# Dividing the first x tile of an interleave kernel between two DMA queues: by columns or by partitions

## The chip, the cores and the metric

The kernel runs on one core of a Trainium2 chip. The metric is the device time of one launch in microseconds (us). Three runs of the kernel before took 314.11 to 314.35 us, with a median of 314.26 us.

## The reference

Two fp32 arrays, x and y, of shape (32, 256, 1024) are interleaved element by element along the last axis into one array of shape (32, 256, 2048):

```python
result = np.zeros((batch, seq, dim * 2), dtype=np.float32)
result[..., 0::2] = x
result[..., 1::2] = y
```

Each input has 33.55 MB and the output 67.11 MB, so 134.22 MB go between off-chip memory and the core. There is no arithmetic.

## The kernel before

Each input is seen as a flat array and cut into n = 8 tiles of 128 x 8192 elements (4 MiB): a tile is contiguous in memory, and row p of it, one partition, holds 8192 consecutive elements, 32 KiB. Since the interleave acts on the flat order, tile k of x and tile k of y give 128 rows of 16,384 output elements.

On-chip memory holds two x tiles (`xt0`, `xt1`), two y tiles (`yt0`, `yt1`) and two output tiles (`ot0`, `ot1`), each 128 x 8192. Output tile h takes half h of the columns: 4096 columns of x and 4096 of y, woven to 8192.

Three engines work, each through its own list, with counting semaphores between them. A DMA adds 16 to its semaphore when it has landed; a copy adds 1 to `woven`.

- SyncE (the SP queue) issues the loads (lines 47 to 55): for each k the x tile (line 52) and then the y tile (line 55). From k = 2 on it first waits until VectorE has read the old content of the buffer.
- VectorE (lines 57 to 70) takes, for each k and for h = 0 and 1, the x half-columns into the even places of `ot[h]` (line 67) and the y half-columns into the odd places (line 70). Before line 67 it waits for the x tile (`xsem`, only at h = 0) and from k = 1 on for the store that last read `ot[h]` (`osem`). Before line 70, at h = 0, it waits for the y tile (`ysem`).
- ScalarE (the ACT queue, lines 72 to 78) waits for each finished `ot[h]` and issues its store (line 76). The very first store is cut in two parts, 1 MiB and 3 MiB.

The first x tile is special. It is loaded by two DMAs, one from each queue (lines 45 and 46), which take one half of the columns of all 128 rows each: 128 pieces of 16 KiB. The part from the ACT queue has a semaphore of its own, `hsem`. VectorE waits for `xsem` before the first copy (h = 0), which needs only the first column half, and for `hsem` before the copy of the second (h = 1).

After the lists are built, `tile_interleave_kernel` takes the first DMA of SyncE and of ScalarE, which are these two, and moves them to the opening of the program, ahead of the barrier that the engines pass at the start.

Of the kernel before, what the change touches and what calls it, by code (L numbers as in the profile page):

```python
# [3 lines left out]


def _interleave(nc, x, y, out):
    P = 128
    W = 8192
    H = W // 2  # L10

    total = 1
    for s in x.shape:
        total *= s
    n = total // (P * W)
    assert n * P * W == total

    def rows(ap, names, k):
        flat = ap.rearrange("b s d -> (b s d)")
        return flat[k * names : (k + 1) * names].rearrange("(p w) -> p w", p=P)  # L20

    fp32 = mybir.dt.float32
    xt = [nc.alloc_sbuf_tensor(f"xt{b}", [P, W], fp32).ap() for b in (0, 1)]
    yt = [nc.alloc_sbuf_tensor(f"yt{b}", [P, W], fp32).ap() for b in (0, 1)]
    ot = [nc.alloc_sbuf_tensor(f"ot{b}", [P, W], fp32).ap() for b in (0, 1)]

    xsem = [nc.alloc_semaphore(f"xsem{b}") for b in (0, 1)]
    hsem = nc.alloc_semaphore("hsem")
    ysem = [nc.alloc_semaphore(f"ysem{b}") for b in (0, 1)]
    woven = nc.alloc_semaphore("woven")  # L30
    osem = [nc.alloc_semaphore(f"osem{b}") for b in (0, 1)]

    xs = [rows(x, P * W, k) for k in range(n)]
    ys = [rows(y, P * W, k) for k in range(n)]
    os_ = [rows(out, 2 * P * W, k) for k in range(n)]

    Q = W // 4

    def parts(k, h):
        return [slice(0, W)] if k or h else [slice(0, Q), slice(Q, W)]  # L40

    def stored(k, h):
        return 16 * sum(len(parts(j, h)) for j in range(k))

    nc.sync.dma_start(out=xt[0][:, :H], in_=xs[0][:, :H]).then_inc(xsem[0], 16)
    nc.scalar.dma_start(out=xt[0][:, H:], in_=xs[0][:, H:]).then_inc(hsem, 16)
    for k in range(n):
        b = k % 2
        if k >= 2:
            nc.sync.wait_ge(woven, 4 * (k - 2) + 3)  # L50
        if k:
            nc.sync.dma_start(out=xt[b], in_=xs[k]).then_inc(xsem[b], 16)
        if k >= 2:
            nc.sync.wait_ge(woven, 4 * (k - 2) + 4)
        nc.sync.dma_start(out=yt[b], in_=ys[k]).then_inc(ysem[b], 16)

    for k in range(n):
        b = k % 2
        for h in (0, 1):
            c = slice(h * H, (h + 1) * H)  # L60
            if h == 0:
                nc.vector.wait_ge(xsem[b], 16 * (k // 2 + 1))
            elif k == 0:
                nc.vector.wait_ge(hsem, 16)
            if k:
                nc.vector.wait_ge(osem[h], stored(k, h))
            nc.vector.tensor_copy(out=ot[h][:, 0::2], in_=xt[b][:, c]).then_inc(woven, 1)  # L67
            if h == 0:
                nc.vector.wait_ge(ysem[b], 16 * (k // 2 + 1))
            nc.vector.tensor_copy(out=ot[h][:, 1::2], in_=yt[b][:, c]).then_inc(woven, 1)  # L70

    for k in range(n):
        for h in (0, 1):
            nc.scalar.wait_ge(woven, 4 * k + 2 * h + 2)
            for c in parts(k, h):
                nc.scalar.dma_start(
                    out=os_[k][:, h * W : (h + 1) * W][:, c], in_=ot[h][:, c]
                ).then_inc(osem[h], 16)

    nc.scalar.wait_ge(osem[0], stored(n, 0))  # L80
    used = sorted(s.num for s in [*xsem, hsem, *ysem, woven, osem[0]])
    assert used == list(range(used[0], used[-1] + 1)), used
    nc.scalar.sem_clear(range(used[0], used[-1] + 1))
    nc.sync.nop(nofuse=True).wait_op(osem[1], stored(n, 1), "sem-ge").then_inc(
        osem[1], -stored(n, 1)
    )


def kernel(tc, x, y, out):
    nc = tc.nc  # L90
    tc.close()
    tc.compile()

    _interleave(nc, x, y, out)

    blocks = nc.main_func.blocks
    for engine in (mybir.EngineType.SP, mybir.EngineType.Activation):
        opening = blocks[0].instructions
        at, moved = next(
            (b, i)  # L100
            for b in blocks[1:]
            for i in b.instructions
            if i.engine == engine and i.opcode == "DMACopy"
        )
        assert not (moved.sync_info and moved.sync_info.on_wait)
        body = at.instructions
        body.remove(moved)
        gate = next(
            n
            for n, i in enumerate(opening)  # L110
            if i.engine == engine and i.opcode == "Drain"
        )
        opening.insert(gate, moved)
        at.instructions = body
        blocks[0].instructions = opening


# [1 line left out]
_INS = ['x', 'y']  # L119
_OUTS = [((32, 256, 2048), 'float32')]  # L120


# [23 lines left out]
```

## Time and profile before

| Item | Value |
|---|---|
| Median of 3 runs | 314.26 us (314.11 to 314.35) |
| The profiled execution, its own time | 314.21 us |
| Its span in the trace | 312.9 us |
| Busy time of VectorE | 71.9 us (23% of the span), 32 copies |
| A copy at line 67, at line 70 | 2295 ns, 2288 ns |
| Read and written by the DMA engines | 67.11 MB and 67.11 MB, 429 GB/s over the span |
| Chain that ended last | DMA 82%, DVE 12% |
| First store issued, last store issued | 24.35 us, 298.04 us |

The page cuts the span into 40 slices and gives each engine's busy share in tenths; the DMA row is the mean of the core's 16 DMA engines. The two DMA queues are q1, which has SyncE's loads, and q10, which has ScalarE's stores and one half of the first x tile. In the list of DMA issues, the time is from the issue to the landing of the whole transfer. In the timeline, a row of SPq or ACTq is the issue of a DMA and not its transfer. A view by stretches adds up bytes by whole packets, so that its GB/s and its DMA share can be some per cent off in a short stretch.

### The profile page before, as it was taken

The page shows a single profiled execution, that of the slowest core. Times are in us where ns is not written, and L with a number is a line of the kernel's source. Part 1 is how long each engine was busy: PE and PEld are TensorE (multiplying, and loading weights), DVE is VectorE, ACT ScalarE, POOL GpSimd, SP SyncE. Part 2 cuts the span into 40 slices and gives each one's busy share as a digit, 9 for nine tenths or more (in the row PEclk, how much of TensorE's full clock was granted, in tenths as well). Part 3 has the DMA queues.
Part 4 walks back from the last instruction along what each step waited for, and adds up shares of the span by engine and source line. Part 5 has one row for each costly group of instructions (what it writes and reads, how often), then busy time and mean ns, then how long its engine had stood idle before and what let it go on. Part 6 is the DMA issues. An engine that isn't in the chain of part 4 may idle for free.

```text
span 312.9 us, 114 instructions
## 1 busy us (share of the span) xinstructions
DVE 71.9 (23%) x32; POOL 0.2 (0%) x4
## 2 busy tenths in 40 slices
DVE  0216000501305023050230503205032050415400
POOL 0000000000000000000000000000000000000000
DMA  8999999999999999999999999999999999999998
GB/s 344 461 406 431 436 402 431 440 465 406 448 423 431 440 406 465 402 469 402 469 402 465 406 457 415 436 436 419 452 402 469 402 469 402 469 402 461 411 444 360
DMA packets 4896, 134.22 MB, mean 429 GB/s; under 512 B 544, under 2 KB 544, under 8 KB 544
## 3 DMA queue, kind: packets, MB, share of 16 engines
q10 hardware_dynamic: 2592, 69.21, 51.3%
q1 hardware_dynamic: 2304, 65.01, 48.5%
HBM read 67.11 MB, written 67.11 MB: 429 GB/s over the span
## 4 chain that ended last, share of the span: by engine, by line
DMA 82%; DVE 12%; issue 0%
DMA out_dram<-ot 76%; DMA yt<-in_y_dram 7%; DVE ot L70 6%; DVE ot L67 6%
## 5 line engine op out<-in xcount | busy, mean ns | idle before, releaser
L67 DVE COPY ot<-xt 128x4096 f32<-128x4096 f32 x16 | 36.7, 2295 | 218.0 <-DMA out_dram<-ot 206.3
L70 DVE COPY ot<-yt 128x4096 f32<-128x4096 f32 x16 | 36.6, 2288 | 8.0 <-DMA yt<-in_y_dram 8.0
L130 POOL MEMSET const-uint8-127<- 128x1 uint8 x1 | 0.1, 102 | 0.0
L130 POOL MEMSET const-bfloat16-1.0<- 128x1 bf16 x1 | 0.1, 101 | 0.0
L130 POOL MEMSET const-float32-0.0<- 128x1 f32 x1 | 0.1, 98 | 0.2 <-issue 0.2
L130 POOL MEMSET const-float32-1.0<- 128x1 f32 x1 | 0.1, 98 | 0.0
## 6 DMA issues: line engine op xcount, KB each, us to landing
out_dram<-ot ACTq DMA_DIRECT2D x15, 4096.0 KB, 34.1
yt<-in_y_dram SPq DMA_DIRECT2D x8, 4096.0 KB, 41.5
xt<-in_x_dram SPq DMA_DIRECT2D x7, 4096.0 KB, 24.4
out_dram<-ot ACTq DMA_DIRECT2D x1, 3072.0 KB, 32.8
xt<-in_x_dram SPq DMA_DIRECT2D x1, 2048.0 KB, 11.7
xt<-in_x_dram ACTq DMA_DIRECT2D x1, 2048.0 KB, 13.4
out_dram<-ot ACTq DMA_DIRECT2D x1, 1024.0 KB, 16.1
```

Source lines behind the costliest of these rows:

```text
L67: nc.vector.tensor_copy(out=ot[h][:, 0::2], in_=xt[b][:, c]).then_inc(woven, 1)
L70: nc.vector.tensor_copy(out=ot[h][:, 1::2], in_=yt[b][:, c]).then_inc(woven, 1)
L130: nc = _bacc.Bacc("TRN2", target_bir_lowering=False, num_devices=1)
```

## The change

The first x tile is still loaded by two DMAs, one from each queue, 2 MiB each, but the cut runs across the partitions: the SP queue's DMA takes rows 0 to 63 and the ACT queue's rows 64 to 127, each with whole rows of 32 KiB. Since the first copy (h = 0) reads all 128 rows, it now needs both DMAs, so the wait for `hsem` stands ahead of it, together with the wait for `xsem`; the wait ahead of the h = 1 copy goes.

```diff
-    nc.sync.dma_start(out=xt[0][:, :H], in_=xs[0][:, :H]).then_inc(xsem[0], 16)
-    nc.scalar.dma_start(out=xt[0][:, H:], in_=xs[0][:, H:]).then_inc(hsem, 16)
+    nc.sync.dma_start(out=xt[0][: P // 2], in_=xs[0][: P // 2]).then_inc(xsem[0], 16)
+    nc.scalar.dma_start(out=xt[0][P // 2 :], in_=xs[0][P // 2 :]).then_inc(hsem, 16)
...
             if h == 0:
                 nc.vector.wait_ge(xsem[b], 16 * (k // 2 + 1))
-            elif k == 0:
-                nc.vector.wait_ge(hsem, 16)
+                if k == 0:
+                    nc.vector.wait_ge(hsem, 16)
             if k:
                 nc.vector.wait_ge(osem[h], stored(k, h))
```

## The prediction

> **What bounds the kernel now.** I read the page first for who is busy, then the DMA rows, then the start of the timeline, the waits and the chain.
>
> From the page, the tenths of busy time and the queues:
>
> ```profile
> DVE  0216000501305023050230503205032050415400
> DMA  8999999999999999999999999999999999999998
> ...
> q10 hardware_dynamic: 2592, 69.21, 51.3%
> q1 hardware_dynamic: 2304, 65.01, 48.5%
> ```
>
> The 16 DMA engines are busy from the first slice to the last: the two queues' packets take 51.3 + 48.5 = 99.8% of the time that 16 engines have in the span. VectorE works 71.9 us of 312.9. So the kernel ends when 134.22 MB have gone through, and a lost DMA microsecond anywhere is a microsecond at the end. Next, what the DMA engines move per second (columns: stretch, its length, DVE busy, POOL busy, clock, DMA share, GB/s):
>
> ```profile
> 0.00:1.00 1.00, 0.00 (x0) 0.20 (x4) 1.00 0.07 16
> 1.00:3.00 2.00, 0.00 (x0) 0.00 (x0) 1.00 1.07 311
> 3.00:11.00 8.00, 0.00 (x0) 0.00 (x0) 1.00 1.01 432
> ...
> 100.00:290.00 190.00, 45.78 (x21) 0.00 (x0) 1.00 1.00 433
> ```
>
> Two things are to be seen. The stretch 3 to 11 us moves only the first x tile, in rows of 16 KiB, all loads; the stretch 100 to 290 us moves rows of 32 KiB, loads and stores mixed. Both run at 432 to 433 GB/s, which is 433 / 16 = 27.06 GB/s for each engine. Row length and direction do not matter; some path of fixed rate, one per engine, is full. And the start is slow: by 3.00 us, 16 + 2 x 311 = 638 KB have been moved where 433 GB/s would give 1299, so 661 KB, or 1.53 us, are lost there, about 1.0 us of it before the first byte.
>
> The start itself, from the timeline and the waits:
>
> ```profile
> 0.00 0.37 SPq L45 DMA_DIRECT2D xt<-in_x_dram  x1
> 0.12 0.37 ACTq L46 DMA_DIRECT2D xt<-in_x_dram  x1
> ...
> 11.70 2.30 DVE L67 COPY ot<-xt 128x4096 f32<-128x4096 f32 x1 [11.70 <-DMA xt<-in_x_dram]
> 22.02 2.29 DVE L70 COPY ot<-yt 128x4096 f32<-128x4096 f32 x1 [8.02 <-DMA yt<-in_y_dram]
> ```
>
> ```profile
> xt<-in_x_dram SPq DMA_DIRECT2D x1, 2048.0 KB, 11.7
> xt<-in_x_dram ACTq DMA_DIRECT2D x1, 2048.0 KB, 13.4
> ```
>
> The halves of the first x tile land at 11.7 and at 0.12 + 13.4 = 13.5 us. Each is 2.097 MB, or 4.84 us at 433 GB/s; had one been served whole before the other, it would have landed near 7 us. So the engines serve the two queues in turns, and both halves are in flight from end to end. The first y tile, issued third, lands at 22.0, and VectorE stands 8.0 us for it. The chain of waits starts with that transfer and is from there almost all stores:
>
> ```profile
> 1.57 20.43 DMA yt<-in_y_dram
> ...
> 28.75 48.06 DMA out_dram<-ot
> ```
>
> **The change, part by part.**
>
> *The wait on hsem moves from the second x copy to the first.* The first L67 copy now waits for both halves. In the present landing times it would start at 13.5 instead of 11.7 and end at 15.8. Queued behind it on VectorE is the first L70 copy, which cannot start before y lands at 22.0: 6.2 us of cover. If that cover were gone, the cost would be up to one copy, 2.3 us, in the first store; but even this would not reach the end by itself, because behind y the SP queue already holds the next x and y tiles, 8.39 MB or 19.4 us of work for the DMA engines. I cost it at nothing. The second L67 copy loses a wait that had long been met: nothing.
>
> *Rows of 32 KiB instead of 16.* 128 packets of the first x tile instead of 256, the same 4.194 MB. The two rows above give the same rate for both lengths: nothing in the steady flow. A gain can come only from the slow start; of its 1.53 us, 1.0 us precedes any data and is untouched, so the bound below nothing is 0.5 us. I take nothing.
>
> *Issue.* Two DMA issues as before, at the same places in the opening (the code that moves the first DMA of SP and ACT there takes the new ones alike): nothing.
>
> *Each transfer spans 64 rows instead of 128.* This is the cost that no row of the trace shows; every transfer in it spans all 128 rows. With 128 rows over 16 engines each engine has 8 rows; with 64, each has 4, and the 16 engines together address one half of the rows of on-chip memory. The measured limit of 27.06 GB/s can belong to the engine or to the path into its group of rows. The trace cannot part the two, as each engine has always had a group of rows to itself.
> - If it belongs to the engine, the 8 packets that each engine moves for this tile (4 from each queue) take 8 x 32,768 B / 27.06 GB/s = 8 x 1.211 = 9.69 us, as now. Cost: nothing.
> - If it belongs to the rows' path, a half has 8 paths for 16 engines. While all engines work on SP's half, two share each path and a packet takes 2.42 us; when all turn to ACT's half, the same holds of the other 8 paths, while the first 8 lie idle. Then the tile takes 19.38 us: cost 9.69 us, all of it on the path that sets the end, since the y tile and everything behind it queue on the same engines.
>
> The second case has one relief. Two engines on one path are not exactly in step. At each change of queue the one ahead is for a moment alone on the new path, and the other alone on the old one. The order of turns follows from the two issues: SP's came 0.12 us earlier, so about S S A S A S A A, with five changes. The lead can be between nothing and the spread of the start, the 0.5 us of slow start after the first byte; I take 0.2 us as my estimate, nearer to the lower end, because every later packet has the same rate and nothing makes the lead grow. That gives back 5 x 0.2 = 1.0 us.
>
> I take the second case. A rate that is the same for loads and stores, and for rows of 16 and of 32 KiB, points to the one thing common to them all, the way into and out of the rows on the chip; the engine alone would explain it too, which is why the other case keeps a chance. And the strict sharing of turns seen above, with both queues starting within 0.12 us, puts all engines on the same half at the same time.
>
> [...]
>
> **The sum.** The profiled execution took 314.21 us, span 312.9 and 1.3 around it, 0.05 under the median of 314.26, so I work from it: 314.21 + 9.69 - 1.0 = 322.9 us. Nothing makes up for it later: the DMA engines have no idle time in which to catch up, and the loop's waits are all for stores.
>
> What is late next: both halves land at about 22 us, the first x copy runs beside the y transfer, y lands near 30.7, and from there the timeline is that of before, shifted by 8.7 us.
>
> **The rivals.** A measurement of this kernel tells about 0.2%, 0.6 us, from no change.
>
> 1. *No loss, 314.2 (13%).* The rate belongs to the engine, or the engines that share a path fall fully out of step, one on SP's half while the other is on ACT's; then all 16 paths are in use. For it: both halves are in flight all the time, so traffic for all 128 rows is always there. Against it: all engines begin on SP's half, and nothing in the rows pushes them apart. It decides if the first x copy starts at about 13.5 us. The time is then that of before, within 0.3 us, because the moved wait is covered by 6.2 us.
> 2. *Partly out of step, 315.5 to 321, middle 318 (17%).* The same sharing of paths, but the lead grows from turn to turn until a good part of the turns overlap: half of 9.69 is 4.8 us lost, hence about 318 to 319. For it: packets of 2.42 us are long, and an arbiter need not be even. Against it: the same as above.
> 3. *Four engines to a path, 343 (3%).* If the 64 rows are dealt out singly, so that in one turn only 4 paths are in use, the tile takes 4 x 9.69 = 38.8 us, 29 us more. Against it: it needs a dealing by single rows, while with 128 rows the full rate shows that neighbouring engines don't collide.
> 4. *Faster, 313.5 (3%).* The slow start shrinks because half as many, longer packets are set up. Its bound is the 0.5 us found above, 0.7 us with all the noise between runs (314.11 to 314.35), and the rows show no cost of a packet's own.
>
> **How the numbers follow.** The forecast, two engines to a path nearly in step, has 64%. Its own range: a lead of nothing gives 323.9, with 0.4 us for the start 324.3; a lead of 0.5 us gives 314.21 + 9.69 - 2.5 = 321.4, rounded to 321.0. To reach 8 in 10 the range takes in rival 2, with 17%: 315.5 to 324.3, which leaves out the 13%, 3% and 3%. Slower by over 0.2%: 64 + 17 + 3 = 84%. Within 0.2%: 13%. Faster: 3%.
>
> **What would show it.** Right: in the stretch 3 to 11 us the DMA share stays at about 1.0 while GB/s falls to some 220 to 240; the two halves land at about 20 to 22 us after issue instead of 11.7 and 13.4; L67's wait for x grows to about 22 us, L70's wait for y stays at 6 to 8 us; from 40 us on every row of the timeline is moved by one constant of about 8.7 us; the GB/s of the steady part stay at 433. Wrong: 432 GB/s in that stretch and an x wait of 13.5 us (rival 1); about 110 GB/s (rival 3). If the stretch runs at half the rate but the end does not move, the reading that the DMA engines are full throughout is wrong. If the first loads are as fast as before and the end is later, the loss is in the moved wait, and the cover was misjudged.

## The result, and the profile after

The changed kernel takes 323.59 us (323.5 to 323.7) against 314.22 us (314.11 to 314.35) for the kernel before in the same session: 9.37 us longer, a ratio of 1.0298 with a 95% interval of 1.0283 to 1.0313. The forecast was 322.9, the range 315.5 to 324.3.

The page of the changed kernel, the tenths and GB/s of its 40 slices of 8.06 us, and the landing times of the first x tile:

```profile
span 322.4 us, 115 instructions
...
DMA  9999999999999999999999999999999999999998
GB/s 195 236 285 398 455 443 403 447 451 394 455 443 403 455 443 403 455 443 403 455 439 407 455 427 419 455 427 419 455 415 431 455 411 435 455 407 439 455 398 382
...
xt<-in_x_dram SPq DMA_DIRECT2D x1, 2048.0 KB, 19.8
xt<-in_x_dram ACTq DMA_DIRECT2D x1, 2048.0 KB, 23.2
```

The GB/s row of the kernel before, in slices of 7.82 us:

```profile
GB/s 344 461 406 431 436 402 431 440 465 406 448 423 431 440 406 465 402 469 402 469 402 465 406 457 415 436 436 419 452 402 469 402 469 402 469 402 461 411 444 360
```

The DMA engines look just as busy as before, in the first slices too; only the GB/s row tells that the first three slices moved 51 to 70% as much. The view by stretches, columns as before:

```profile
3.00:11.00 8.00, 0.00 (x0) 0.00 (x0) 1.00 0.96 205
...
100.00:290.00 190.00, 44.97 (x20) 0.00 (x0) 1.00 1.00 433
```

```profile
3.00:21.00 18.00, 0.00 (x0) 0.00 (x0) 1.00 1.01 222
```

The rate falls from 432 to 205 GB/s from 3 to 11 us, and over the whole of the tile to 222 at a share of 1.01, or 220 GB/s for engines that are exactly full. The tile's 4.194 MB take 19.08 us at that rate and 9.69 us at 433: 9.39 us more, close to the measured loss of 9.37. The steady part is untouched.

The trace also records the packets one by one; a packet is here one row of the tile, moved by one DMA engine. The queue rows of two stretches of 2.42 us, 5.80 to 8.22 and 8.22 to 10.64 us (queue, packets begun, MB, their time as a share of 16 engines' time):

```profile
q10 hardware_dynamic: 16, 0.52, 99.7%
...
q1 hardware_dynamic: 16, 0.52, 99.4%
```

All 16 engines begin one packet of ScalarE's half, and then one of SyncE's, and each packet takes 2.41 us, twice the 1.21 us of a row of 32 KiB in the kernel before: a busy engine is here one that waits with a packet in hand. Joined end to end, the packets of each of the 16 engines come in the order S S A S A S A A (S for SyncE's half, A for ScalarE's). A packet that follows one of the same half takes 2.56 us (median), a packet that follows one of the other half 2.40 to 2.41.

The timeline and the chain of waits:

```profile
23.45 2.29 DVE L67 COPY ot<-xt 128x4096 f32<-128x4096 f32 x1 [23.45 <-DMA xt<-in_x_dram]
31.87 2.29 DVE L70 COPY ot<-yt 128x4096 f32<-128x4096 f32 x1 [6.13 <-DMA yt<-in_y_dram]
```

```profile
2.12 29.73 DMA yt<-in_y_dram
...
279.94 2.30 DVE ot L67
```

The same late step in the chain of the kernel before:

```profile
270.46 2.30 DVE ot L67
```

The first copy of y starts at 31.87 instead of 22.02 us, 9.85 later; late in the run (279.94 against 270.46) the same step of the chain is 9.48 us behind. VectorE still waits 6.1 us for y after its first x copy, so the moved wait is covered.

### The profile page after: what moved, and what is told of

It is laid out like the page before. It is cut to its first block, busy times and chain, and to the rows that moved or that the text cites. A ratio compares the mean times of both kernels' runs of the same rounds, so it can differ in the third digit from the quotient of the medians.

```text
span 322.4 us, 115 instructions
## 1 busy us (share of the span) xinstructions
DVE 72.0 (22%) x32; POOL 0.2 (0%) x4
## 4 chain that ended last, share of the span: by engine, by line
DMA 83%; DVE 12%; issue 0%
DMA out_dram<-ot 74%; DMA yt<-in_y_dram 9%; DVE ot L70 6%; DVE ot L67 6%
## 5 line engine op out<-in xcount | busy, mean ns | idle before, releaser
L67 DVE COPY ot<-xt 128x4096 f32<-128x4096 f32 x16 | 36.7, 2295 | 229.4 <-DMA out_dram<-ot 206.0
L70 DVE COPY ot<-yt 128x4096 f32<-128x4096 f32 x16 | 36.6, 2289 | 6.1 <-DMA yt<-in_y_dram 6.1
## 6 DMA issues: line engine op xcount, KB each, us to landing
xt<-in_x_dram SPq DMA_DIRECT2D x1, 2048.0 KB, 19.8
xt<-in_x_dram ACTq DMA_DIRECT2D x1, 2048.0 KB, 23.2
```

## The experiments

Theory: a transfer of 64 neighbouring rows reaches only half of the paths into on-chip memory, and 16 engines share eight. Rivals: the moved wait costs the time; the source, now two regions of 2 MiB, is slow to read; the two queues' turns are at fault; the loss belongs to the start of the program.

**Only the wait.** The kernel before, with the changed order of waits:

```diff
-            elif k == 0:
-                nc.vector.wait_ge(hsem, 16)
+                if k == 0:
+                    nc.vector.wait_ge(hsem, 16)
```

> The first x tile by column halves as before; only the wait for hsem stands ahead of the first copy, as in the changed kernel. Paths theory (a transfer of 64 rows reaches half of the paths into on-chip memory, and 16 engines share 8): 314.2 us, within 0.3; the first L67 starts at about 13.5 us, L70 still at 22.0. Wait theory (the moved wait costs the time): 320 us or more.

Measured: 314.29 us, ratio 1.0001 (0.9992 to 1.0011). L67 starts at 13.99 us, L70 still waits 6.12 us for y. The wait costs nothing.

**Only the source.** The column halves of before, read from the two contiguous halves of the tile, which leaves the first tile's data in another order:

```diff
-    nc.sync.dma_start(out=xt[0][:, :H], in_=xs[0][:, :H]).then_inc(xsem[0], 16)
-    nc.scalar.dma_start(out=xt[0][:, H:], in_=xs[0][:, H:]).then_inc(hsem, 16)
+    def near(h):
+        flat = x.rearrange("b s d -> (b s d)")
+        return flat[h * P * H : (h + 1) * P * H].rearrange("(p w) -> p w", p=P)
+
+    nc.sync.dma_start(out=xt[0][:, :H], in_=near(0)).then_inc(xsem[0], 16)
+    nc.scalar.dma_start(out=xt[0][:, H:], in_=near(1)).then_inc(hsem, 16)
```

> The two first DMAs write the same places as before (column halves of all 128 rows), but each reads one contiguous half of the tile in off-chip memory, 2 MiB, as the changed kernel's do; the first x tile's data are thereby in another order. Paths theory: 314.2 us, 432 GB/s from 3 to 11 us. Source theory (a region of 2 MiB read by all engines at once is slow): about 323.6 us, 205 to 230 GB/s from 3 to 20 us.

Measured: 314.28 us, ratio 1.0000 (0.9991 to 1.0009), 428 GB/s from 3 to 11 us. Reading a narrow region is not slow; what is left is the side where the rows are written: how many rows a transfer has, or which.

**Both halves on one queue.**

```diff
-    nc.scalar.dma_start(out=xt[0][P // 2 :], in_=xs[0][P // 2 :]).then_inc(hsem, 16)
+    nc.sync.dma_start(out=xt[0][P // 2 :], in_=xs[0][P // 2 :]).then_inc(hsem, 16)
...
-    for engine in (mybir.EngineType.SP, mybir.EngineType.Activation):
+    for engine in (mybir.EngineType.SP, mybir.EngineType.SP):
```

The second part keeps both DMAs in the opening.

> The row halves of the changed kernel, both issued by SyncE one behind the other, none by ScalarE. Paths theory: at least as slow as the changed kernel, 323.6 to 324.8 us, because there is one change from half to half in place of five and so less relief; about 205 to 215 GB/s until 21 us. Rival (the loss comes from two queues taking turns): 314.2 us.

Measured: 324.19 us, ratio 1.0318 (1.0301 to 1.0335). The stretch of the tile:

```profile
3.00:21.00 18.00, 0.00 (x0) 0.00 (x0) 1.00 1.00 206
```

So two queues do not cause the loss; their turns give back a little of it, 0.60 us of time and 206 to 220 GB/s, or 7%. The packets say where: with one queue there is one change of half, and the packet behind it takes 2.41 us where the others take 2.56; with two queues there are five. Four more changes at 0.15 us are the 0.60.

**Half of the bytes in narrow transfers.** The first column half over all rows, the second as two transfers of 64 rows:

```diff
-    nc.scalar.dma_start(out=xt[0][:, H:], in_=xs[0][:, H:]).then_inc(hsem, 16)
+    for r in (slice(0, P // 2), slice(P // 2, P)):
+        nc.scalar.dma_start(out=xt[0][r, H:], in_=xs[0][r, H:]).then_inc(hsem, 16)
...
-                nc.vector.wait_ge(hsem, 16)
+                nc.vector.wait_ge(hsem, 32)
...
```

Here and below, the lines left out of a diff move the new DMAs to the opening or fit a wait's count to them.

> The first column half by one DMA over all 128 rows from SyncE, as before; the second column half by two DMAs of 64 rows from ScalarE. Half of the tile's bytes are in transfers of 64 rows. Paths theory: half of the loss, 314.2 + 4.7 = 318.9 us (318 to 319.5). Rival (a fixed cost of any transfer of 64 rows at the start): 323.6 us, or 314.2 if only the long rows of 32 KiB matter.

Measured: 320.48 us (319.19 to 321.08), ratio 1.0192 (1.0167 to 1.0218). The loss lies between none and that of the changed kernel, as a dose should, but it is 6.2 us and not 4.7: two thirds for half of the bytes. SyncE's transfers over all rows are slowed along with the narrow ones: from 6 to 11 us its packets of 16 KiB take 1.07 us on average, where the kernel before has 0.61, and from 13.5 to 21 us those of y, of 32 KiB, 1.75 instead of 1.21. Why the sum comes to 6.2 us is open.

**A tile in the middle of the run.** The x tile k = 4 as two transfers of 64 rows, the first as before:

```diff
-        if k:
+        if k == 4:
+            for r in (slice(0, P // 2), slice(P // 2, P)):
+                nc.sync.dma_start(out=xt[b][r], in_=xs[k][r]).then_inc(xsem[b], 16)
+        elif k:
             nc.sync.dma_start(out=xt[b], in_=xs[k]).then_inc(xsem[b], 16)
...
```

> The first x tile as before; the fifth (k = 4), in the middle of the run, is loaded by two DMAs of 64 rows on the SP queue. Paths theory: the engines are full there too, and each of 8 packets per engine takes about 1.2 us longer if the engines are in step: up to 314.2 + 9.7 = 323.9; less, down to 316, if between the stores they fall out of step. Rival (the loss belongs to the start of the program): 314.2 us.

Measured: 322.38 us, ratio 1.0249 (1.0212 to 1.0287). The loss, 8.1 us, is not one of the start. The trace, where the load is issued at 117.9 us:

```profile
105.00:115.00 10.00, 0.00 (x0) 0.00 (x0) 1.00 0.98 423
...
125.00:135.00 10.00, 0.00 (x0) 0.00 (x0) 1.00 1.02 321
135.00:145.00 10.00, 4.50 (x2) 0.00 (x0) 1.00 1.01 357
```

Beside stores of all rows, too, the share stays at 1.0 and the rate drops for the time of the load.

**A store.** The store k = 4, h = 0 as two transfers of 64 rows:

```diff
+            if (k, h) == (4, 0):
+                for r in (slice(0, P // 2), slice(P // 2, P)):
+                    nc.scalar.dma_start(
+                        out=os_[k][r, :W], in_=ot[h][r]
+                    ).then_inc(osem[h], 16)
+                continue
...
```

> Loads as before; one store of 4 MiB in the middle (k = 4, h = 0) is divided into two DMAs of 64 rows on the ACT queue. If the paths bind a store's reading as they bind a load's writing: 318 to 324 us. If only writing into on-chip memory is bound: 314.2 us.

Measured: 317.35 us (315.87 to 318.29), ratio 1.0080 (1.0045 to 1.0114): below the span that was expected if reading is bound as writing is, and above none. The group of stores timed below settles that reading is bound too (204 GB/s for 64 neighbouring rows, 426 for every second row). Here most of the narrow packets were not slowed: in the trace, of an execution of 316.40 us, the first 48 of the store's 128 packets take turns with load packets and take 1.21 us, the next 16 follow store packets directly and take 1.86, and the last 64 take 1.22, again in turns with loads. So beside loads a narrow store is hardly bound; why is not shown.

**Rows that are not neighbours.** The changed kernel with the even rows on one queue and the odd rows on the other:

```diff
-    nc.sync.dma_start(out=xt[0][: P // 2], in_=xs[0][: P // 2]).then_inc(xsem[0], 16)
-    nc.scalar.dma_start(out=xt[0][P // 2 :], in_=xs[0][P // 2 :]).then_inc(hsem, 16)
+    nc.sync.dma_start(out=xt[0][0::2], in_=xs[0][0::2]).then_inc(xsem[0], 16)
+    nc.scalar.dma_start(out=xt[0][1::2], in_=xs[0][1::2]).then_inc(hsem, 16)
```

> The changed kernel, but SyncE's DMA takes the 64 even rows and ScalarE's the 64 odd rows, so that each transfer reaches over all 128 partitions. Reach theory (a transfer is bound by the paths that its rows reach in all): full rate, 314.2 us. Turn theory (what counts is how many paths the 16 engines use at one time, and with 4 rows each they may still be two to a path): up to 323.6 us; between the two if only some of the turns collide.

Measured: 315.24 us (314.63 to 316.19), ratio 1.0031 (1.0020 to 1.0043). 64 rows of 32 KiB in each transfer, twice, as in the changed kernel; only which rows go together differs, and 1.05 of the 9.37 us are left.

```profile
3.00:11.00 8.00, 0.00 (x0) 0.00 (x0) 1.00 1.07 459
11.00:22.00 11.00, 2.30 (x1) 0.00 (x0) 1.00 0.99 429
```

The first copy of y starts at 22.14 us, 0.12 behind the kernel before. The rest of its 1.05 us comes later, between about 25 and 117 us (in the trace, of an execution of 315.58 us, the copy that starts at 57.60 us in the kernel before is 2.07 us late, and those from 115.57 us on 1.37), and varies from run to run; its cause was not sought.

**Sets of rows by themselves.** Ahead of the kernel before, groups of four DMAs with a wait behind each, so that nothing else moves:

```diff
+    four = [*yt, *ot]
...
+    for j, t in enumerate(four):
+        nc.sync.dma_start(out=t[0:64], in_=xs[j][0:64]).then_inc(psem, 16)
+    nc.sync.wait_ge(psem, 128)
...
```

> Ahead of the kernel before, SyncE issues 17 groups of four DMAs each, loads of 14 sets of rows and stores of three, with rows of 32 KiB, and waits for each group; the first x loads are not moved to the opening. A group's time, from its first issue to the next group's, is some 2 us and the packets of one engine one behind the other. At the rate of the kernel before (1.21 us each): all 128 rows 32 packets, 39 us; 64 rows 16, 19 us; 32 rows 8, 10 us; 16 or 8 rows 4, 5 us; 1 row 4, 5 us. Engine theory: these times hold whatever the rows. Paths theory: rows 0 to 63 and rows 64 to 127 each take double, 39 us; and eight or sixteen neighbouring rows, which crowd on few paths, take a multiple of 5 us. [...] Stores: the same doubling for 64 rows if the paths bind reading too, none if not.

The launch takes 711.3 us with its groups. The view by stretches, cut inside each group; the groups are in order rows 0:128, 0:64, 64:128, 0:128:2, 0:32, 0:128:4, 0:16, then 0:8 and 0:32:4, then stores of 0:128, 0:64 and 0:128:2:

```profile
5.00:40.00 35.00, 0.00 (x0) 0.00 (x0) 1.00 1.01 434
47.00:84.00 37.00, 0.00 (x0) 0.00 (x0) 1.00 0.97 198
90.00:128.00 38.00, 0.00 (x0) 0.00 (x0) 1.00 0.97 198
133.00:150.00 17.00, 0.00 (x0) 0.00 (x0) 1.00 1.00 432
155.00:173.00 18.00, 0.00 (x0) 0.00 (x0) 1.00 0.97 198
178.00:185.00 7.00, 0.00 (x0) 0.00 (x0) 1.00 1.01 435
190.00:206.00 16.00, 0.00 (x0) 0.00 (x0) 1.00 0.91 98
...
236.00:252.00 16.00, 0.00 (x0) 0.00 (x0) 1.00 0.46 49
...
269.00:273.00 4.00, 0.00 (x0) 0.00 (x0) 1.00 0.44 172
...
296.00:332.00 36.00, 0.00 (x0) 0.00 (x0) 1.00 1.02 437
338.00:374.00 36.00, 0.00 (x0) 0.00 (x0) 1.00 0.99 204
380.00:396.00 16.00, 0.00 (x0) 0.00 (x0) 1.00 0.99 426
```

The DMA share says how many of the 16 engines hold a packet (1.01 for all rows, 0.46 for 8 rows), GB/s, by the paths theory, how many paths carry it: all of them at 434, somewhat under half for either half of the rows (198), about a quarter for 16 neighbours (98), an eighth for 8 neighbours (49). Eight rows spread by four go at 172 instead of 49. A limit of the engine alone is out: 0:64 and 0:128:2 would then go at the same rate. From the first issue of a group to that of the next, by the timeline:

| Rows | Time, us | Packets of one engine, at 1.21 us | Time less 2.05 us, over that |
|---|---|---|---|
| 0:128 | 41.27 | 32, 38.7 us | 1.0 |
| 0:64, 64:128 | 43.54, 43.29 | 16, 19.4 us | 2.1, 2.1 |
| 0:128:2 | 22.20 | 16, 19.4 us | 1.0 |
| 0:32 | 22.63 | 8, 9.7 us | 2.1 |
| 0:128:4 | 12.34 | 8, 9.7 us | 1.1 |
| 0:16 | 20.86 | 4, 4.8 us | 3.9 |
| 0:64:4, 0:128:8 | 12.72, 12.68 | 4, 4.8 us | 2.2, 2.2 |
| 0:8 | 20.57 | 4, 4.8 us | 3.8 |
| 0:16:2, 0:128:16 | 12.39, 12.33 | 4, 4.8 us | 2.1, 2.1 |
| 0:32:4 | 7.85 | 4, 4.8 us | 1.2 |
| 0:1 | 6.89 | 4, 4.8 us | 1.0 |
| stores 0:128, 0:64, 0:128:2 | 40.35, 42.59, 21.17 | 32, 16, 16 | 1.0, 2.1, 1.0 |

The third column is an estimate: the packets that one engine has of a group's four DMAs if the rows are dealt out evenly, one row at least to each engine that works, at the 1.21 us of the kernel before. The 2.05 us of the fourth are an estimate of a group's fixed time, from the group of one row: 6.89 us less four packets of 1.21. What is left comes near one, two or four times the third column: one for 0:128, 0:128:2, 0:128:4 and 0:32:4, two for either half, for 0:32 and for four sets that are spread, four for 0:16 and 0:8. By the paths theory that is the number of engines that share a path. Which rows share one, the groups do not settle: 0:128:8 and 0:128:16 have no neighbours and take twice the time too. Where the factor is two, a packet takes 2.56 us (median, as in 0:64 and 0:32), longer than twice 1.21; where it is four, as in 0:16 and 0:8, 4.82 us, four times 1.21 and no more. 64 rows take 43.54 us, as long as all 128 with 41.27, and bring half.

**Engines out of step.** The prediction held that two halves in flight do not fill all paths because all engines turn to the same half at the same time. In the changed kernel they do, as its packets show. One extra DMA of 8 rows ahead of the halves was to put eight engines a packet behind:

```diff
+    nc.sync.dma_start(out=ot[1][0:32:4], in_=xs[1][0:32:4]).then_inc(hsem, 16)
     nc.sync.dma_start(out=xt[0][: P // 2], in_=xs[0][: P // 2]).then_inc(xsem[0], 16)
...
```

> The changed kernel, with one more DMA ahead of its two: 8 rows of 32 KiB (0.26 MB, rows of another x tile that nothing reads, into 8 rows of an output tile that is overwritten later, rows 0, 4, .. 28), from SyncE. If 8 rows go to 8 of the 16 engines, one each, these start the halves about one packet (1.2 us) behind the other 8. Paths theory with engines in step: the two engines of a path then work on different halves most of the time and the loss goes, if the pairs are made of one engine with the extra row and one without: 314.2 + 1.2 = 315.4 us (315 to 317). If the pairs lie within the same 8, no relief: 324 to 325. Rival (8 paths are all that 64 rows can use, whatever the order): 324 to 325.

> Control for the run with engines out of step: the kernel before (column halves) with the same extra DMA of 8 rows, and a wait for it ahead of the second copy. All theories: 314.2 plus the time of the extra rows, between 0.6 us (0.26 MB over 16 engines) and 1.2 us (one row on each of 8 engines): 314.8 to 315.5.

Measured: 326.27 us, ratio 1.0370 (1.0338 to 1.0402), and for the control on column halves 316.76 us, ratio 1.0071 (1.0047 to 1.0095); the control was 1.3 us slower than expected. The difference of the two, 9.51 us, is the loss of the changed kernel again: no relief. The extra DMA had a flaw as a test: it takes SyncE 0.79 us to issue, and ScalarE's half was first in line. So it was tried with the extra DMAs alone in the opening, one and then two of them, and the halves issued by both queues behind the barrier:

> The row halves of the changed kernel, behind one extra DMA of 8 rows (rows 0, 4, .. 28; by the groups timed before, eight paths and one packet on each of 8 engines), which alone is moved to the opening; the halves are issued by both queues behind the barrier, some 1.6 us later. Eight engines are still at their extra packet when the other eight begin on a half. If the eight come out on the other half than the rest, and each path is shared by one engine of either eight, the two halves fill all 16 paths and most of the loss goes: 317 to 319 us with the extra rows and the later issue. If the turns stay in step, or the sharing engines lie within one eight, or halves cannot overlap at all: 325 to 328 us.

> The same with two extra DMAs of 8 rows ahead (into two tiles), so that eight engines lag by about one more packet. With relief: 318 to 321 us; without: 326 to 330 us. If relief shows in one of the two kernels and not in the other, the order of turns decides; if in neither, sharing out of step is not to be had in this way.

Measured: 326.44 us, ratio 1.0390 (1.0372 to 1.0407), and 326.53 us, ratio 1.0391 (1.0375 to 1.0406). In the traces the halves are issued at 2.14 and 2.86 us instead of 0.00, which is near the 2.85 and 2.94 us that these kernels lose beyond the changed one. From 11 to 20 us they ran at 211 and 233 GB/s, or 222 and 220 for engines that are exactly full. With one extra DMA the engines did come out of step: for 68% of the time from the first to nearly the last packet of ScalarE's half, at least five engines were on each half, against 10% in the changed kernel. Yet a packet still took 2.35 us (median) instead of 2.41. With two extra DMAs they were out of step for only 22% of it. So engines in step are not what keeps the paths from being filled, or not alone. It may be that the engines that share a path lag together; the traces do not name the engine of a row, and this stays open.

## Why the prediction was right, by its own steps

- *What bounds the kernel.* Right in the main. What a load lost showed at the end, at the start of the run (y 9.85 us late, the end 9.37) and in the middle (8.1). That nothing makes up for it later is not quite so: of the 9.85 us, 0.45 came back by 67 us, where the shift is 9.40; the cause was not sought.
- *The moved wait, the longer rows, the issue: nothing.* Right for the wait (314.29); the narrow source, a term that the prediction does not name, costs nothing either (314.28). Long rows and issue together cost 0.12 us at the landing of y by the even and odd rows; the other 0.9 us of that run may belong to them or not. A transfer of 64 rows takes 0.54 us to issue instead of 0.37 at line 45, and y's issue moves from 1.57 to 2.12 us, which is hidden, with the queues full. But the tile's own first packets begin 0.37 us later (1.52 against 1.14 us, the mean of 16 engines), a term that was put at nothing.
- *64 rows reach half of the paths.* Right, and the step on which all hung. The trace of before could not part it from a limit of the engine; the set 0:128:2 at 432 GB/s against 0:64 at 198 does. That there are 16 paths, and 8 for a half, is the prediction's estimate from 16 engines with 8 rows each; the runs show the factor of two and not the number.
- *The size.* Forecast 9.69 - 1.0 = 8.7 us; y came 9.85 late and the end 9.37. The terms in us, for one engine (mean of 16):

  | Term | Forecast | By the packets |
  |---|---|---|
  | the tile's packets, after | 19.38 - 1.0 = 18.38 | 19.51 |
  | the tile's packets, before | 9.69 | 10.51 |
  | later begin of the tile | 0 | 0.37 |
  | y's first packet, longer | 0 | 0.45 |
  | loss by then | 8.69 | 9.82 |

  The relief of 0.2 us at each change of half was not there: a packet behind a change took 2.41 us, the full rate of a shared path, and one without a change 2.56. Before, the tile's first packets are slow (1.27 us where the later ones take 0.61); the prediction left this start as it was, but the changed kernel's first packets took 2.37 us, no more than shared ones do. The first y packet took 1.66 us instead of 1.21, beside the last packets of the tile. That the forecast came within 0.7 us of the end is in part luck, for these terms, and the 0.45 us that came back, partly cancel.
- *Why two halves do not fill all paths.* The engines were in step, in the very order of turns that was forecast, with five changes. But this is not shown to be the reason: with one extra DMA ahead, out of step for 68% of the time, the packets still took 2.35 us. The number did not need the reason to be right, only that there is little relief.
- *What would show it.* The stretch 3 to 11 us was forecast at 220 to 240 GB/s and read 205; over the whole tile 222. The halves landed 19.8 and 23.2 us after issue (forecast 20 to 22), L67 waited 23.4 us (22), L70 6.1 (6 to 8), and the shift is constant from 67 us on, at 9.4 to 9.5 us (forecast: from 40 us on, at 8.7). The rivals with no loss, with four engines to a path throughout and with a faster start are out; a good part of the turns overlapping, at 318, too.

## What to carry to other kernels

The rate of a DMA by itself was set here by which rows it has (64 neighbouring rows at 198 GB/s, every second row at 432); by the paths theory, by the fullest path among them. So divide a tile between queues by columns or by interleaved rows (314.22 and 315.24 us), and not by halves of the partitions (323.59); two halves in flight together did not make up for it. The busy share of the DMA engines does not show this fault, since an engine that waits with a packet in hand counts as busy (a share of 1.01 at 222 GB/s): read GB/s beside it, stretch by stretch. Where DMA is the bound from end to end, a single tile of 4 MiB loaded so cost 9.4 us at the start and 8.1 in the middle; a store divided so, beside loads, cost 3.1.

## What the runs showed of the hardware that was not expected

Where, by the paths theory, two engines share a path, 6% are lost beyond the sharing itself (for 64 neighbouring rows 198 GB/s at a share of 0.97, or 204 for engines that are exactly full, in place of 216, half of 432; in the stores 204 at a share of 0.99), but at a change of half, and where four engines share one, nothing is lost (2.41 and 4.82 us a packet, of 1.21 alone). 32 rows spread by four get the full 435 GB/s, more than twice the 198 of 64 neighbouring rows: how many rows a transfer has matters less than which. And beside transfers over all rows, narrow ones cost more than their bytes for a load (6.2 us where 4.7 was expected) and less for a store (3.1 us): stores of 64 rows that take turns with loads ran at 1.21 us a packet, where stores alone took 2.55.
